# One decoder layer on one core: sixteen instead of eight of the 32 hidden tiles of the second feed-forward product by seven products of quarters

## The chip, the core and the metric

The kernel runs on one core of one Trainium2 chip. The metric is the device time of one launch in microseconds (us). Engines are named as the profile names them: PE is TensorE (PEld its weight loads), DVE is VectorE, ACT is ScalarE, POOL is GpSimd, SP is SyncE, on which every DMA of this kernel is issued.

## The reference, cut to what matters

The layer mixes tokens (a gated unit and sparse attention), attends to 256 memory tokens, and ends in a dense feed-forward block, which is what the change touches. There are 512 tokens of width 1024 and 4096 hidden columns, all float32:

```python
h = rms_norm(x, norm_ffn_g[l])
x = x + jnp.square(jax.nn.relu(h @ w_ff1[l])) @ w_ff2[l]
```

## The kernel before

Every float32 operand of a product is split into a rounded part `hi` and a remainder `lo` (`split_any`: a cast on ACT or DVE, then a subtraction on DVE), and a product is three matmuls: hi·hi, hi·lo, lo·hi.

The 4096 hidden columns are 32 tiles `f` of 128. The first product writes them transposed (`hid[f]`, 128 hidden columns by 512 tokens). Tiles 4 to 31 of the first product are already made in groups of four by `seven`.

The second product (stage `ff2`) has two ways. **Plain**: `load_ff2` loads 128 rows of `w_ff2` into a `raw` buffer and splits them and `hid[f]`; `part` adds the tile's product to eight accumulators in PSUM (`accs`: four token tiles by two column halves). One tile is 24 matmuls that stream 512 columns each. **By quarters**: eight hidden tiles at once. `quarters` cuts their 1024 hidden columns by 512 tokens into four quarters a11, a12, a21, a22 and makes seven split operands from them: A11, A12, A22 themselves, and S1 = a21+a22, S2 = S1−a11, S3 = a11−a21, S4 = a12−S2. `seven` then runs, for each half `g` of the output columns, seven products instead of eight (24 matmuls of 256 columns each, by `prod2`). It forms sums of the weight quarters (`either_tt`, DVE or POOL) and splits them (`pair`), adds the products up from PSUM on DVE (`u2`, `v`), and hands four results to `sink`, which multiplies by the row factor `rf[t]`, adds to the residual and stores to `out`.

Tiles 8 to 15 (`SEVEN = 8`) go by quarters, the 24 others plain, in the sequence `order`. The quarters are prepared after the twelfth plain tile. At the end come the plain tiles' accumulators, added to the residual `xr`, and then the two groups `fg0` and `fg1`.

Buffers come from shared pools: `b8` has 12 buffers of 8 KB a partition, `w` four (split weights), `raw` three, `P` six and `bT` two of 512 columns. A hidden tile or an operand in a `b8` buffer must have been read for the last time before the next one gets it.

Nothing runs in the order of the code. `Plan` records all operations and `schedule` lays them out per engine in advance. Among the operations that could start first on an engine it takes the one with the smallest due number, which is its place in the code, shifted by `LEADS` of its stage. Engines then run their rows strictly in that order, so a row that waits holds back all behind it, on SP too.

Of the kernel before, what the change touches and what calls it, by code (L numbers as in the profile page):

```python
# [9 lines left out]
F32 = mybir.dt.float32  # L10
# [4 lines left out]
OP = mybir.AluOpType  # L15
AX = mybir.AxisListType

P = 128
# [19 lines left out]
SEVEN = 8  # L38
# [19 lines left out]
         "wa": dict(w=3, raw=2),  # L58
         "wf": dict(w=1, raw=1)}

LEADS = {"ch_f0": -4441, "ch_f1": 6232, "ch_norm0": -2300, "ch_norm1": -2363, "ch_norm2": 367,
# [9 lines left out]
         "ln": -7310, "masks": -496, "mem": -4549, "mix": -620, "mk": -3102, "mkv": -2398,  # L71
# [10 lines left out]


class Plan:
# [338 lines left out]
def hybrid_block(ctx, tc, x, mem, norm_mix_g, w_in, sg_ln_g, sg_ln_b, sg_w, sg_b, q_norm_g,  # L423
# [66 lines left out]
    def split_any(src, hi, lo):  # L490

        nc.either(("scalar", "copy"), ("vector", "tensor_copy"))(hi, src)
        dve.tensor_tensor(lo, src, hi.bitcast(F32), OP.subtract)
# [869 lines left out]
    def hid_tiles(f):  # L1363

        if f < 2:
            return [zpool.tile([P, 512], F32, tag="bT", bufs=2, name=nm("hid")) for _ in range(2)]
        if f < 8:
            return [zpool.tile([P, 512], F32, tag="P", bufs=6, name=nm("hid")) for _ in range(6)]
        if f < 20:
            t = b8([P, 4, T], F32)  # L1370
            hid4[f] = t
            return [t[:, i, :] for i in range(4)]
        t = [zpool.tile([P, 2, 512], F32, tag="q", bufs=5, name=nm("hid")) for _ in range(1 if f == 28 else 2)]
        if f == 28:
            g = cpool.tile([P, 2, 512], F32, tag="gain", bufs=1, name=nm("hid"))
            nc.home[g.tensor.name] = "gain"
            t.append(g)
        return [v[:, i, :] for v in t for i in range(2)]

    def hid_tile(f):  # L1380
# [42 lines left out]
    def half(t, i):  # L1423
        return t[:, i, :].rearrange("p (k n) -> p k n", k=4)

    def either_tt(out, a, b, op):
        nc.either(("vector", "tensor_tensor"), ("gpsimd", "tensor_tensor"))(out, a, b, op)
# [127 lines left out]
            start=f == order[0], stop=f == order[-1])  # L1555


    def quarters():
        t = b8([P, 2, 1024], F32)
        nc.stage = "fs"  # L1560
        a11, a12, a21, a22 = (hid4[SEVEN + 4 * kh][:, :, th * 2 * P:th * 2 * P + 2 * P]
                              for th in range(2) for kh in range(2))

        def parts(src, name):
            nc.stage = f"fs.{name}"
            w = b8([P, 2, 1024], F32R)
            h = half(w, 0), half(w, 1)
            split_any(src, *h)
            return h

        A11 = parts(a11, 0)
        either_tt(half(t, 0), a21, a22, OP.add)
        S1 = parts(half(t, 0), 1)
        either_tt(half(t, 1), half(t, 0), a11, OP.subtract)
        S2 = parts(half(t, 1), 2)
        either_tt(half(t, 0), a11, a21, OP.subtract)
        S3 = parts(half(t, 0), 3)
        A12 = parts(a12, 4)
        either_tt(half(t, 0), a12, half(t, 1), OP.subtract)
        S4 = parts(half(t, 0), 5)  # L1580
        A22 = parts(a22, 6)
        return t, (A11, A12, None, A22, S1, S2, S3, S4)

# [10 lines left out]
                nc.tensor.matmul(o, al[:, k, c], wh[:, k, :], **dict(on, stop=i == 1 and k == 3))  # L1594


    order = [*range(20, 28), *range(SEVEN), *range(SEVEN + 8, 20), *range(28, 32)]
    for n, f in enumerate(order[:-LAST]):
        nc.stage = "ff2"
        load_ff2(f)  # L1600
        for t in range(TT):
            for blk in range(2):
                part(f, t, blk)
        if n == 11:
            tq, quads = quarters()
    nc.stage = "ff2"
    for f in order[-LAST:]:
        load_ff2(f)
    nc.stage = "xr"
    xr = [b8([P, 2, D], F32) for _ in range(2)]  # L1610
    for t in range(TT):
        dma(xr[t // 2][:, t % 2, :], xq[t])
    nc.stage = "ff2"
    for t in range(TT):
        for blk in range(2):
            for f in order[-LAST:]:
                part(f, t, blk)
            xv = xr[t // 2][:, t % 2, blk * 512:blk * 512 + 512]
            dve.scalar_tensor_tensor(xv, accs[2 * t + blk], rf[t], xv, OP.mult, OP.add)

    for g in range(2):
        def load_w(kh, ch):
            t = raw4()
            c = g * 512 + ch * 2 * P
            dma(t.rearrange("p (k n) -> p k n", k=4), w2v[:, SEVEN + 4 * kh:SEVEN + 4 * kh + 4, c:c + 2 * P])
            return t

        def sink(src, th, ch):
            for i in range(2):
                t = 2 * th + i  # L1630
                c = g * 512 + ch * 2 * P
                xv = xr[t // 2][:, t % 2, c:c + 2 * P]
                dve.scalar_tensor_tensor(xv, src[:, i * 2 * P:i * 2 * P + 2 * P], rf[t], xv, OP.mult, OP.add)
                dma(out[0, t * P:t * P + P, c:c + 2 * P], xv)

        seven(f"fg{g}", load_w, tq[:, g, :], prod2, quads, [bank() for _ in range(4)], sink)
    nc.issue()


# [29 lines left out]
```

## Time and profile before

| | |
|---|---|
| time, median of 3 runs | 680.83 us (680.05 to 682.28) |
| profiled execution: its time, its span | 681.13 us, 679.4 us |
| PE busy | 670.3 us, 99% |
| DVE busy | 527.9 us, 78% |
| ACT busy | 360.2 us, 53% |
| POOL busy | 79.3 us, 12% |
| mean granted clock of TensorE | 0.999 |

The span runs from the first to the last instruction, and the 1.7 us to the time lie around it. A matmul's duration in the profile holds its way through the array, so durations of neighbours overlap; busy time counts an overlap once. The feed-forward part fills the second half: its first product ends at about 504 us, the plain tiles of the second end at 635.4 us, and the two groups by quarters at 675.7 us.

### The profile page before, as it was taken

Reading aid. Unit: us, or ns where it says so; the run is one execution under the profiler, and the core shown is the slowest. Engines: PE = TensorE matmul, PEld = TensorE weight load, DVE = VectorE, ACT = ScalarE, POOL = GpSimd, SP = SyncE. Lnnn points to the kernel's source line nnn. Section 1 sums busy time; section 2 is a strip of 40 time slices with the busy share of each in tenths; the row PEclk is TensorE's granted clock in tenths of the full one; section 3 lists DMA queues with packets and bytes.
Section 4 is the critical chain, followed back from the end, with each engine's and each line's share of the span. In section 5 each row is a group of like instructions: output and inputs, shape, how many; then the busy total and the mean of one; then the engine's idle time right before and its main releaser. Section 6 shows DMA issues by size and latency. Waiting matters only on the chain.

```text
span 679.4 us, 11076 instructions
## 1 busy us (share of the span) xinstructions
PE 670.3 (99%) x4232; PEld 601.8 (89%) x4232; DVE 527.9 (78%) x940; ACT 360.2 (53%) x690; POOL 79.3 (12%) x123
## 2 busy tenths in 40 slices
PE   8999999899999999999999999999999999999997
PEld 7898888788989898898899999999998888888997
DVE  6688889898989996578899979888998344444695
ACT  5444576786877784566635645456583221121330
POOL 2001211053343230031200000000000000000000
PEclk9999999999999999999999999999999999999999
DMA  8633465451111210305332334433253623222231
GB/s 257 201 89 107 142 180 182 157 185 63 63 64 63 67 53 9 122 1 156 125 94 63 114 105 124 124 94 113 74 170 110 217 93 94 93 94 93 73 115 63
DMA packets 54453, 74.80 MB, mean 110 GB/s; under 512 B 3392, under 2 KB 38720, under 8 KB 54400
## 3 DMA queue, kind: packets, MB, share of 16 engines
q1 hardware_dynamic: 54400, 74.10, 34.9%
q8 instruction: 33, 0.54, 0.3%
q14 instruction: 20, 0.16, 0.1%
HBM read 69.89 MB, written 4.19 MB: 109 GB/s over the span
## 4 chain that ended last, share of the span: by engine, by line
PE 93%; DMA 2%; DVE 2%; ACT 1%; POOL 0%; issue 0%; SPq 0%; DVEq 0%; ACTq 0%; POOLq 0%
PE ps L419 93%; DMA raw<-in_cmp_w_dram 2%; DVE b L419 1%; DVE w L419 1%; DMA b<-in_x_dram 1%; ACT w L419 1%; ACT L419 0%; POOL P L419 0%; ACT b L419 0%; SPq L419 0%; ACT pc L419 0%; DVE q L419 0%; DVE P L419 0%; DVEq L1664 0%; DVE pt L419 0%
## 5 line engine op out<-in xcount | busy, mean ns | idle before, releaser
L419 PE MATMUL ps<-w,b 128*128 128x512 f32 (+3 forms) x1312 | 261.7, 353 | 0.5 <-DVE w L419 0.5
L419 PEld LDWEIGHTS ps<-w,b 128*128 128x128 f32 (+1 forms) x1312 | 210.2, 188 | 29.8 <-DVE w L419 1.0
L419 ACT CAST w<-raw 128x1024 fp32r<-128x1024 f32 (+1 forms) x89 | 90.9, 1022 | 132.0 <-PE ps L419 124.3
L419 PE MATMUL ps<-b,w 128*128 128x256 f32 (+1 forms) x1224 | 152.8, 287 | 0.0
L419 PEld LDWEIGHTS ps<-b,w 128*128 128x128 f32 x1224 | 150.3, 192 | 1.9
L419 DVE TENSOR_TENSOR w<-raw,w 128x1024 fp32r<-128x1024 f32 (+2 forms) x109 | 127.9, 1174 | 27.1 <-ACT w L419 26.2
L419 PE MATMUL ps<-w,q 128*128 128x512 f32 x624 | 148.4, 392 | 0.0
L419 PEld LDWEIGHTS ps<-w,q 128*128 128x128 f32 x624 | 116.0, 188 | 23.2
L419 DVE TENSOR_TENSOR b<-ps,b 128x512 fp32r<-128x512 f32 (+2 forms) x88 | 54.2, 637 | 9.1 <-ACT b L419 8.7
L419 ACT CAST b<-ps 128x512 fp32r<-128x512 f32 (+2 forms) x88 | 46.0, 546 | 20.2 <-PE ps L419 19.8
L419 PE MATMUL ps<-b,b 128*128 128x256 f32 (+1 forms) x344 | 54.1, 288 | 0.0
L419 ACT CAST w<-b 128x1024 fp32r<-128x1024 f32 x21 | 22.0, 1049 | 49.4 <-PE ps L419 37.2
L419 PEld LDWEIGHTS ps<-b,b 128*128 128x128 f32 x344 | 46.4, 190 | 2.0 <-DVE b L419 0.2
L419 POOL TENSOR_SCALAR P<-P,s,gates 128x128 f32<-128x128 f32 (+3 forms) x57 | 35.6, 633 | 69.7 <-DVE s L419 65.4
L419 DVE TENSOR_TENSOR w<-b,w 128x1024 fp32r<-128x1024 f32 x27 | 32.9, 1220 | 10.9 <-ACT w L419 10.8
L419 ACT ACTIVATE P<-P,s 128x128 f32<-128x128 f32 (+3 forms) x64 | 35.7, 559 | 6.9 <-DVE s L419 6.7
L419 DVE TENSOR_TENSOR z<-ps,z 128x512 f32<-128x512 f32 (+2 forms) x54 | 34.7, 646 | 4.5 <-PE ps L419 4.0
L419 POOL TENSOR_TENSOR b<-raw,b 128x1024 f32<-128x1024 f32 x1 | 2.4, 2400 | 278.3 <-DVE w L419 278.3
L419 PE MATMUL ps<-b,q 128*128 128x256 f32 (+2 forms) x144 | 33.3, 343 | 0.0
L419 PE MATMUL ps<-idf,P 128*128 128x128 f32 x192 | 31.8, 275 | 0.5 <-POOL P L419 0.5
L419 POOL TENSOR_TENSOR r<-s,negh 128x1 f32<-128x1 f32 (+2 forms) x25 | 19.6, 784 | 108.8 <-DVE s L419 108.8
L419 DVE CUSTOM_DVE_ANT_0 P<-ps,tri 128x128 f32<-128x128 f32 (+3 forms) x64 | 28.8, 482 | 1.4 <-PE ps L419 1.1
(166 smaller groups left out, 667.9 us busy)
## 6 DMA issues: line engine op xcount, KB each, us to landing
raw<-in_w_ff_dram SPq DMA_DIRECT2D x64, 512.0 KB, 3.8
raw<-in_w_in_dram SPq DMA_DIRECT2D x12, 512.0 KB, 3.7
raw<-in_cmp_w_dram SPq DMA_DIRECT2D x8, 512.0 KB, 5.0
raw<-in_w_out_dram SPq DMA_DIRECT2D x8, 512.0 KB, 3.5
raw<-in_w_mkv_dram SPq DMA_DIRECT2D x8, 512.0 KB, 3.6
b<-in_x_dram SPq DMA_DIRECT2D x8, 256.0 KB, 6.0
raw<-in_w_in_dram SPq DMA_DIRECT2D x8, 256.0 KB, 6.2
b<-in_x_dram SPq DMA_DIRECT2D x4, 512.0 KB, 4.3
```

The lines of the kernel that those rows point to most:

```text
L419: getattr(getattr(self.nc, eng), op)(*a, **k)
```

## The change

The second product takes tiles 16 to 23 by quarters too. `quarters(f)` and the groups run for f = 8 and f = 16, so there are four groups (`fg8`, `fg9`, `fg16`, `fg17`) and 16 plain tiles. The first set's operands are prepared after the sixth plain tile. The second set's stand in the code behind the first group. Tiles 20 to 23 lie in two buffers of two tiles each, so an operation on their quarters becomes two of 512 columns (`pieces`). The residual no longer waits in two `b8` buffers; it lies in eight of 512 columns (`bT`, `P`) and is loaded by eight DMAs instead of four. The sums of the groups with f = 8 stay in these buffers, those with f = 16 go to `out`. `LEADS` is another table.

```diff
-LEADS = {"ch_f0": -4441, "ch_f1": 6232, "ch_norm0": -2300, "ch_norm1": -2363, "ch_norm2": 367,
...
+LEADS = {"ch_f1": -603, "ch_f2": -578, "ch_f3": -4970, "ch_norm2": 876, "ch_o0": -494, "ch_o0.w0.2": -1640,
...
-    def quarters():
+    def quarters(f):
+
         t = b8([P, 2, 1024], F32)
-        nc.stage = "fs"
-        a11, a12, a21, a22 = (hid4[SEVEN + 4 * kh][:, :, th * 2 * P:th * 2 * P + 2 * P]
+        a11, a12, a21, a22 = ([(k, v[:, :, th * 2 * P:th * 2 * P + 2 * P]) for k, v in hid4[f + 4 * kh]]
                               for th in range(2) for kh in range(2))
...
+        def tt(out, a, b, op):
+            for o, x, y in pieces(out, a, b):
+                either_tt(o, x, y, op)
+
         A11 = parts(a11, 0)
-        either_tt(half(t, 0), a21, a22, OP.add)
-        S1 = parts(half(t, 0), 1)
...
+        tt(t0, a21, a22, OP.add)
+        S1 = parts(t0, 1)
+        tt(t1, t0, a11, OP.subtract)
+        S2 = parts(t1, 2)
...
-    order = [*range(20, 28), *range(SEVEN), *range(SEVEN + 8, 20), *range(28, 32)]
+    order = [*range(SEVEN + 16, 28), *range(SEVEN), *range(28, 32)]
...
-        if n == 11:
-            tq, quads = quarters()
+        if n == 5:
+            tq, quads = quarters(SEVEN)
...
-    xr = [b8([P, 2, D], F32) for _ in range(2)]
+    xr = [[zpool.tile([P, 512], F32, tag=tag, bufs=n, name=nm("xr")) for _ in range(2)]
+          for tag, n in (("bT", 2), ("P", 6), ("P", 6), ("P", 6))]
     for t in range(TT):
-        dma(xr[t // 2][:, t % 2, :], xq[t])
+        for blk in range(2):
+            dma(xr[t][blk], xq[t][:, blk * 512:blk * 512 + 512])
...
+    for f in (SEVEN, SEVEN + 8):
+        for g in range(2):
+            def load_w(kh, ch):
+                t = raw4()
                 c = g * 512 + ch * 2 * P
-                xv = xr[t // 2][:, t % 2, c:c + 2 * P]
-                dve.scalar_tensor_tensor(xv, src[:, i * 2 * P:i * 2 * P + 2 * P], rf[t], xv, OP.mult, OP.add)
-                dma(out[0, t * P:t * P + P, c:c + 2 * P], xv)
...
+            def sink(src, th, ch):
+                for i in range(2):
+                    t = 2 * th + i
+                    c = ch * 2 * P
+                    xv = xr[t][g][:, c:c + 2 * P]
+                    dve.scalar_tensor_tensor(xv, src[:, i * 2 * P:i * 2 * P + 2 * P], rf[t], xv, OP.mult, OP.add)
+                    if f > SEVEN:
+                        dma(out[0, t * P:t * P + P, g * 512 + c:g * 512 + c + 2 * P], xv)
+
+            seven(f"fg{f + g}", load_w, tq[:, g, :], prod2, quads, [bank() for _ in range(4)], sink)
+            if f == SEVEN and g == 0:
+                tn, next_quads = quarters(f + 8)
+        tq, quads = tn, next_quads
```

On PE, the rows behind the last plain tile of before are whole products of 24 matmuls (the weights `w_...` of one product, the operand `b_...` of the hidden columns, the bank `ps_...`):

```order
L419 MATMUL ps_1169<-w_1248,q_1249 128x512 x3
L419 MATMUL ps_1252<-w_1258,b_1103_1207 128x256 x24
L419 MATMUL ps_1253<-w_1260,b_1104_1208 128x256 x24
L419 MATMUL ps_1254<-w_1262,b_1105_1209 128x256 x24
L419 MATMUL ps_1255<-w_1264,b_1106_1210 128x256 x24
L419 MATMUL ps_1252<-w_1267,b_1107_1211 128x256 x24
L419 MATMUL ps_1253<-w_1268,b_1108_1212 128x256 x24
```

At the same place of the changed kernel the products of group `fg8` (banks 1234 to 1237) and, further down, of `fg9` (1261 to 1264) lie in pieces between each other:

```order
L422 MATMUL ps_1169<-w_1224,q_1225 128x512 x3
L422 MATMUL ps_1234<-w_1240,b_1085_1189 128x256 x24
L422 MATMUL ps_1235<-w_1242,b_1086_1190 128x256
L422 MATMUL ps_1236<-w_1244,b_1087_1191 128x256
L422 MATMUL ps_1237<-w_1246,b_1088_1192 128x256 x24
L422 MATMUL ps_1236<-w_1244,b_1087_1191 128x256 x23
L422 MATMUL ps_1234<-w_1249,b_1089_1193 128x256 x24
L422 MATMUL ps_1235<-w_1242,b_1086_1190 128x256 x13
L422 MATMUL ps_1261<-w_1267,b_1085_1189 128x256
L422 MATMUL ps_1235<-w_1242,b_1086_1190 128x256 x10
L422 MATMUL ps_1261<-w_1267,b_1085_1189 128x256 x23
L422 MATMUL ps_1262<-w_1269,b_1086_1190 128x256
```

So 192 matmuls of 512 columns are gone ahead of this place, 336 matmuls of 256 columns stand behind it, and a product's first matmul often stands alone among those of another.

On DVE, between the first and the second group of before (`fg0` and `fg1`), these rows stand: weight sums and remainders (`w`, `raw`, `b_1102_1206`), sums of products (`z`), and updates of the residual (`b_1146`, `b_1147`):

```order
L419 TENSOR_TENSOR w_1270<-b_1102_1206,w_1270 128x1024
L419 TENSOR_TENSOR b_1102_1206<-raw_1276,raw_1275 128x1024
L419 TENSOR_TENSOR z_1265<-ps_1255,z_1265 128x512
L419 TENSOR_TENSOR w_1277<-raw_1275,w_1277 128x1024
L419 SCALAR_TENSOR_TENSOR b_1147_1251<-z_1265,rf_950,b_1147_1251 128x256
L419 SCALAR_TENSOR_TENSOR b_1146_1250<-ps_1252,rf_897,b_1146_1250 128x256
L419 SCALAR_TENSOR_TENSOR b_1146_1250<-ps_1252,rf_924,b_1146_1250 128x256
L419 SCALAR_TENSOR_TENSOR b_1147_1251<-z_1265,rf_965,b_1147_1251 128x256
```

In the changed kernel, in the second group (`fg9`), the rows are these, where `b_1149_1253` is the scratch tile of the second set, `b_1153`, `b_1154` and `b_1155` its operands S3, A12 and S4, and `hid_1087`, `hid_1088` hidden tiles 20 to 23:

```order
L422 TENSOR_TENSOR b_1153_1257<-b_1149_1253,b_1153_1257 128x1024
L422 TENSOR_TENSOR w_1271<-b_1084_1188,w_1271 128x1024
L422 TENSOR_TENSOR w_1273<-raw_1266,w_1273 128x1024
L422 TENSOR_TENSOR b_1084_1188<-raw_1275,b_1084_1188 128x1024
L422 TENSOR_TENSOR b_1154_1258<-hid_1087,b_1154_1258 128x512
L422 TENSOR_TENSOR b_1154_1258<-hid_1088,b_1154_1258 128x512
L422 TENSOR_TENSOR b_1149_1253<-hid_1087,b_1149_1253 128x512
L422 TENSOR_TENSOR b_1149_1253<-hid_1088,b_1149_1253 128x512
L422 TENSOR_TENSOR w_1276<-raw_1275,w_1276 128x1024
L422 TENSOR_TENSOR b_1155_1259<-b_1149_1253,b_1155_1259 128x1024
L422 TENSOR_TENSOR z_1251<-ps_1235,z_1245 128x512
L422 TENSOR_TENSOR w_1277<-raw_1270,w_1277 128x1024
```

Here six rows of the second set stand among those that the running groups need. Its operands A11, S1 and S2 stand further up, among the plain tiles, and A22 further down.

On SP, the loads of the residual now stand one by one among the loads of the plain tiles' weights:

```order
L422 DMA raw_1214<-in_w_ff_dram 128x1024
L422 DMA xr_1230<-xq_749 128x512
L422 DMA raw_1217<-in_w_ff_dram 128x1024
L422 DMA xr_1231<-xq_749 128x512
L422 DMA raw_1220<-in_w_ff_dram 128x1024
L422 DMA xr_1232<-xq_750 128x512
L422 DMA raw_1223<-in_w_ff_dram 128x1024
L422 DMA xr_1233<-xq_750 128x512
L422 DMA raw_1238<-in_w_ff_dram 128x4x256
```

Before, four loads of 128 x 1024 stood there, ahead of the weight loads of the last twelve plain tiles; now each waits for a buffer that a hidden tile leaves.

## Rows read from the trace of the kernel before

**Rows 1.** The page: span, then busy us of each engine.

```profile
span 679.4 us, 11076 instructions
...
PE 670.3 (99%) x4232; PEld 601.8 (89%) x4232; DVE 527.9 (78%) x940; ACT 360.2 (53%) x690; POOL 79.3 (12%) x123
```

**Rows 2.** The chain that ended last: start, us and name of its longest piece.

```profile
200.13 475.57 PE ps L419 x3092
```

**Rows 3.** Whom PE waited for in the whole span: us, times, longest.

```profile
PE ps L419 <- DMA b<-in_x_dram: 1.4, 1, 1.4
PE ps L419 <- DVE pc L419: 1.2, 1, 1.2
PE ps L419 <- DVE zero L419: 1.1, 1, 1.1
PE ps L419 <- DVE b L419: 0.7, 2, 0.6
PE ps L419 <- POOL P L419: 0.5, 1, 0.5
PE ps L419 <- DVE w L419: 0.5, 1, 0.5
```

**Rows 4.** Busy time of each engine by stretch.

```profile
core 0: us, PE busy (x) PEld busy (x) DVE busy (x) ACT busy (x) POOL busy (x), PEclk, DMA share, GB/s
0.00:200.00 200.00, 194.72 (x1140) 167.97 (x1140) 166.29 (x408) 130.62 (x285) 44.42 (x75) 1.00 0.46 141
...
330.00:471.00 141.00, 141.00 (x1104) 137.48 (x1103) 126.04 (x142) 75.94 (x127) 3.74 (x5) 1.00 0.33 101
...
540.00:635.40 95.40, 95.40 (x423) 79.04 (x422) 41.28 (x52) 18.12 (x18) 2.40 (x1) 1.00 0.27 89
635.40:675.70 40.30, 40.28 (x336) 40.08 (x335) 32.79 (x42) 12.74 (x14) 0.00 (x0) 1.00 0.32 98
```

**Rows 5.** Groups by shape, 520 to 680 us: count, busy us, mean ns of one.

```profile
L419 PE MATMUL ps<-w,q 128*128 128x512 f32 x432 | 98.1, 389 | 0.0
...
L419 DVE SCALAR_TENSOR_TENSOR b<-z,rf,b 128x256 f32<-128x256 f32 x12 | 5.3, 480 | 0.1
```

**Rows 6.** DVE in order of time, inside the two groups by quarters.

```profile
636.08 1.22 DVE L419 TENSOR_TENSOR w<-b,w 128x1024 fp32r<-128x1024 f32 x1
637.21 1.22 DVE L419 TENSOR_TENSOR w<-raw,w 128x1024 fp32r<-128x1024 f32 x1
...
653.26 0.68 DVE L419 TENSOR_TENSOR z<-ps,z 128x512 f32<-128x512 f32 x1
653.87 1.22 DVE L419 TENSOR_TENSOR b<-raw,b 128x1024 f32<-128x1024 f32 x1
655.00 0.87 DVE L419 SCALAR_TENSOR_TENSOR b<-z,rf,b 128x256 f32<-128x256 f32 x2
655.79 0.68 DVE L419 TENSOR_TENSOR z<-ps,z 128x512 f32<-128x512 f32 x1
```

**Rows 7.** The one POOL subtraction of the feed-forward end, and DVE beside it.

```profile
626.97 2.40 POOL L419 TENSOR_TENSOR b<-raw,b 128x1024 f32<-128x1024 f32 x1 [278.33 <-DVE w L419]
627.47 0.74 DVE L419 SCALAR_TENSOR_TENSOR b<-ps,rf,b 128x512 f32<-128x512 f32 x1
```

**Rows 8.** DMA issues: count, KB each, median us to landing.

```profile
raw<-in_w_ff_dram SPq DMA_DIRECT2D x64, 512.0 KB, 3.8
...
b<-xq SPq DMA_DIRECT2D x4, 512.0 KB, 5.6
```

**Rows 9.** PE and ACT at the start, in order of time.

```profile
5.95 0.68 ACT L419 ACTIVATE b<-ps,gT 128x512 fp32r<-128x512 f32 x1
...
6.83 0.66 PE L419 MATMUL ps<-idf,b 128*128 128x128 f32 x4 [1.36 <-DMA b<-in_x_dram]
...
7.24 4.53 PE L419 MATMUL ps<-w,b 128*128 128x512 f32 x18
```

More of the change, by code (lines that the diff above doesn't have):

```diff
@@ L59 @@
          "wf": dict(w=1, raw=1)}
-LEADS = {"ch_f0": -4441, "ch_f1": 6232, "ch_norm0": -2300, "ch_norm1": -2363, "ch_norm2": 367,
[9 rows of a table removed]
-         "ln": -7310, "masks": -496, "mem": -4549, "mix": -620, "mk": -3102, "mkv": -2398,
[10 rows of a table removed]
+LEADS = {"ch_f1": -603, "ch_f2": -578, "ch_f3": -4970, "ch_norm2": 876, "ch_o0": -494, "ch_o0.w0.2": -1640,
[23 rows of a table added]
 class Plan:
@@ L1370, in hid_tiles @@
             t = b8([P, 4, T], F32)
-            hid4[f] = t
+            hid4[f] = [(0, t)]
             return [t[:, i, :] for i in range(4)]
@@ L1377, in hid_tiles @@
             t.append(g)
+        else:
+            hid4[f] = [(0, t[0]), (2, t[1])]
         return [v[:, i, :] for v in t for i in range(2)]
@@ L1555, in part, with pieces @@
             start=f == order[0], stop=f == order[-1])
-    def quarters():
+    def quarters(f):
         t = b8([P, 2, 1024], F32)
-        nc.stage = "fs"
-        a11, a12, a21, a22 = (hid4[SEVEN + 4 * kh][:, :, th * 2 * P:th * 2 * P + 2 * P]
+        a11, a12, a21, a22 = ([(k, v[:, :, th * 2 * P:th * 2 * P + 2 * P]) for k, v in hid4[f + 4 * kh]]
                               for th in range(2) for kh in range(2))
+        t0, t1 = ([(0, half(t, i))] for i in range(2))
+        def pieces(*srcs):
+            ks = sorted({k for s in srcs for k, _ in s}) + [4]
+            for k, e in zip(ks, ks[1:]):
+                r = []
+                for s in srcs:
+                    b, v = max((x for x in s if x[0] <= k), key=lambda x: x[0])
+                    r.append(v[:, k - b:e - b, :])
+                yield r
         def parts(src, name):
-            nc.stage = f"fs.{name}"
+            nc.stage = f"fs{f}.{name}"
             w = b8([P, 2, 1024], F32R)
             h = half(w, 0), half(w, 1)
-            split_any(src, *h)
-            return h
+            for x, hi, lo in pieces(src, *([(0, v)] for v in h)):
+                split_any(x, hi, lo)
+            return h
+        def tt(out, a, b, op):
+            for o, x, y in pieces(out, a, b):
+                either_tt(o, x, y, op)
         A11 = parts(a11, 0)
-        either_tt(half(t, 0), a21, a22, OP.add)
-        S1 = parts(half(t, 0), 1)
[L1574 to L1577, printed above, removed]
+        tt(t0, a21, a22, OP.add)
+        S1 = parts(t0, 1)
+        tt(t1, t0, a11, OP.subtract)
+        S2 = parts(t1, 2)
+        tt(t0, a11, a21, OP.subtract)
+        S3 = parts(t0, 3)
         A12 = parts(a12, 4)
-        either_tt(half(t, 0), a12, half(t, 1), OP.subtract)
-        S4 = parts(half(t, 0), 5)
+        tt(t0, a12, t1, OP.subtract)
+        S4 = parts(t0, 5)
         A22 = parts(a22, 6)
@@ L1617, in hybrid_block @@
                 part(f, t, blk)
-            xv = xr[t // 2][:, t % 2, blk * 512:blk * 512 + 512]
+            xv = xr[t][blk]
             dve.scalar_tensor_tensor(xv, accs[2 * t + blk], rf[t], xv, OP.mult, OP.add)
[L1621 to L1630, printed above, removed]
-                c = g * 512 + ch * 2 * P
-                xv = xr[t // 2][:, t % 2, c:c + 2 * P]
-                dve.scalar_tensor_tensor(xv, src[:, i * 2 * P:i * 2 * P + 2 * P], rf[t], xv, OP.mult, OP.add)
-                dma(out[0, t * P:t * P + P, c:c + 2 * P], xv)
-        seven(f"fg{g}", load_w, tq[:, g, :], prod2, quads, [bank() for _ in range(4)], sink)
+    for f in (SEVEN, SEVEN + 8):
+        for g in range(2):
+            def load_w(kh, ch):
+                t = raw4()
+                c = g * 512 + ch * 2 * P
+                dma(t.rearrange("p (k n) -> p k n", k=4), w2v[:, f + 4 * kh:f + 4 * kh + 4, c:c + 2 * P])
+                return t
+            def sink(src, th, ch):
[10 more added lines that the diff above has]
+        tq, quads = tn, next_quads
     nc.issue()
```

42 rows, old and new, of the table LEADS are left out of this document.

## The prediction

> **What bounds the kernel now.** I read the page first: PE is busy for 670.3 of 679.4 us [rows 1]. A share near 100% can still hide waits, since a matmul's duration covers its way through the array, so I asked the chain of waits next. Its longest piece is PE alone, 475.6 us from 200.1 us on without a break [rows 2], which takes in the whole feed-forward block. The list of PE's waits agrees: six kinds, 5.4 us together [rows 3], all of them in the first 200 us or just behind. The table by stretch shows the rest [rows 4]. From 330 to 471 us, where the first product runs by seven products, PE is busy 141.0 of 141.0 us, at the full granted clock (1.00), while DVE is busy 126.0 us (89%). In the plain tiles up to 635.4 us DVE needs 41.3 of 95.4 us (43%), and in the two groups by quarters 32.8 of 40.3 us (81%). The clock is at its upper level, 2.4 GHz, in every stretch shown. So only PE's own rows set the end, and time is won by taking columns off PE, as long as DVE keeps up.
>
> **The product, removed and added.** Eight hidden tiles leave the plain way: 8 x 24 = 192 matmuls of 512 columns. The group by shape has 432 of these in 98.1 us [rows 5], 227.1 ns each when overlaps are counted once (the mean of 389 ns counts them twice). Removed: 192 x 0.2271 = 43.6 us. Added are two groups of seven products of 24 matmuls of 256 columns, 336. Exactly as many run behind 635.4 us in the kernel before, in 40.28 us [rows 4], 119.9 ns each. Added: 40.3 us. The product gains **3.3 us**. It is less than the eighth by which the multiplications shrink (5.5 of 43.6 us), because a matmul of half the width takes 53% of the time, not 50%.
>
> The Trainium skill, TensorE: Matmul & The Clock Gate, section Back-to-back issue gap, gives N/2.4 ns plus about 2.5 ns between isolated matmuls of N columns. By it the two widths would be 215.8 and 109.2 ns and the gain 41.4 − 36.7 = 4.7 us. The trace doesn't agree (227.1 and 119.9 ns), and the measurement decides.
>
> **DVE and ACT behind the plain tiles.** The groups' stretch doubles to 4 x 168 = 672 matmuls, 80.6 us. In the order of the changed kernel I counted DVE's rows behind the last update from the plain accumulators: 40 tensor-tensor rows of 1024, 26 of 512, 32 residual updates of 256. From start to start such rows take 1.13 us (636.08 to 637.21), 0.61 us (653.26 to 653.87) and 0.395 us (two in 0.79 from 655.00) [rows 6]. Sum: 45.2 + 15.9 + 12.6 = 73.7 us. The same count of before (17, 10, 16) gives 31.6 us where the table shows 32.8, so I add 3.7%: 76.4 us, 95% of PE's 80.6. That is tighter than before, but it fits. If instead each row held DVE for its whole duration (1.22, 0.68 and 0.48 us [rows 5, 6]), the sum would be 81.9 us, 1.3 us over.
>
> The tightest place is from DVE's row that adds up the end of `fg8`'s S2 product to its row for the end of `fg9`'s S4 product. The list of rows of `fg9` shown above lies in it, with S3, A12 and S4 of the second set. There are 34 rows (15 of 1024, 11 of 512, 8 of 256): 16.9 + 6.7 + 3.2 = 26.8 us, with the 3.7% 27.8 us, by full durations 29.6 us. PE's 236 matmuls there take 28.3 us. So DVE ends between 1.5 us early and 1.3 us late, and nearer to early, since starts, not durations, set the pace in every row I could read. The pieces into which PE's products are cut have little reserve against a late remainder. I charge **0.3 us** for small waits, between 0 (as from 330 to 471 us, at 89% of DVE) and 2.6 (both overruns).
>
> The other rows of the second set (A11, S1, S2, about 7.5 us) stand among the plain tiles, where DVE has over half its time free; without that cover they would come on top of the 76.4 us and PE would wait for some 3 us. ACT gets seven casts more for the second set and one for each pair, but has 12.7 of 40.3 us busy in the groups [rows 4] and stays far from the bound.
>
> **Loads and residual.** The weights' bytes are the same: eight loads of 512 KB for eight tiles, or eight for two groups. The residual is the same 2 MB in eight loads rather than four. A load of weights lands in 3.8 us, one of the residual in 5.6 us [rows 8]; a plain tile takes 24 x 0.2271 = 5.45 us on PE, and three `raw` buffers stand ahead of it. Cost nothing, as long as a residual load doesn't stop SP (rival below). The last stores are the same rows as before, so what follows PE's end stays.
>
> **The other table of leads.** It reorders every engine. Behind 200 us PE has nothing to win. Ahead of it the 5.4 us of waits include 1.1 us for the first operand of all, so at most 4.3 us could come back; a loss isn't bounded by the trace, and I take once the largest wait seen (1.4 us) as its size. One place can be read: PE stands 1.36 us for the second slice of x until 6.83 us, and only then, after four transposes, starts its first products at 7.24 us [rows 9]. In the new order three products of the first slice stand ahead of these transposes. Their operand is written by ACT from 5.95 us for 0.68 us, so they can start near 6.7 us. I take **0.3 us** of gain, and 0 for all else.
>
> **Sum.** −3.3 + 0.3 − 0.3 = −3.3 us. From the profiled execution's 681.13 us that is 677.8 us. That execution lay 0.3 us over the median of 680.83, so for a median I say 677.5 us, 0.5% faster. About 0.3% (2.0 us) is what a measurement of this kernel can tell from no change.
>
> **Rivals.**
> (1) *DVE becomes the bound of the groups.* For it: 95% by starts, 102% by durations. Against it: 89% without a wait in the first product. It would give back 1.3 to 2.6 us: 678.8 to 680.1 us.
> (2) *POOL stops DVE in the tight stretch.* The new order has two POOL subtractions behind the plain tiles' sums instead of one: the old one beside the last plain tiles, and one in `fg16`'s preparation, next to the end of the stretch above. One takes 2.40 us, and before, DVE's update from PSUM ran beside it at its usual 0.74 us [rows 7]. The rows behind it that matter most have PSUM operands too. If rows with two SBUF operands came to stand beside it and had to wait, PE would be late by 2.4 less the 0.5 to 1.5 us in hand: 678.4 to 679.4 us. The Trainium skill, SBUF — State Buffer, section Who interferes with whom, says that a DVE instruction with two SBUF inputs and a GpSimd one that reads SBUF exclude each other, and that the later one stands still until the first is done. The one pair in these rows has a PSUM operand and ran undisturbed, as the page has it; no row here shows the other kind.
> (3) *The residual's loads hold SP* (slower). Each waits for a hidden tile's buffer, and weights queue behind it. With three `raw` buffers PE has about two plain tiles, 10.9 us, in hand; a load held longer than that stops PE by about a tile for each tile of delay. At one tile, 5.45 us: 683.0 us. For it: four residual loads alternate with the last four weight loads of the plain tiles. Against it: the tiles that leave these buffers are split well ahead of their products, as DVE has over half its time free there.
> (4) *The new order opens other waits in the first 200 us*, or closes more. One more of the largest kind gives 678.9 us; half of the 4.3 us closed gives 675.4.
>
> **Chances.** Forecast, with the product's gain mostly whole and the order neutral or better (675.4 to 678.7 us): 0.72. Rival 1: 0.11. Rival 2: 0.05. Rival 4's loss: 0.08. Rival 3: 0.04. The range leaves out rival 3 and thin ends of the others: 675.7 to 680.2 us. Faster by over 0.3%, below 678.8 us: the forecast and some of rivals 2 and 4, 0.74. Same: 0.21. Slower: 0.05.
>
> **What would show it.** Right: PE busy near 667 us with the same six kinds of waits; plain tiles that end near 592 us and groups of 80.6 to 81 us behind them without PE waits over 0.3 us; DVE near 92 to 95% there. Wrong: PE waits for `w` or for DVE's reads of `ps` between `fg9` and `fg16` (rivals 1, 2), PE waits for `w` among the last plain tiles with SP held by `xr` (rival 3), or a first product by quarters that starts at another time than 43.6 us earlier, less what changed ahead of it (rival 4). A width that costs other than 227 and 120 ns would upset the largest term.

## Result, and the profile after

The changed kernel takes 677.38 us (median of ten runs, 676.16 to 679.81), the kernel before 681.96 us on the same chip (ten runs, 680.05 to 683.8). The ratio is 0.9937, with a 95% interval from 0.9919 to 0.9956: 0.6% faster. The forecast was 677.5 us. Its largest term came out, but that the time was met to 0.1 us is partly luck: the measured gain is 4.6 us, where 3.3 us were forecast from a lower start.

The profiled execution of the changed kernel took 679.81 us, the longest of its ten, and a second one, shown below, 676.3 us. Where they part is told under the experiments. The page of the profiled one, which answers to [rows 1]:

```profile
span 678.0 us, 11433 instructions
...
PE 669.6 (99%) x4376; PEld 609.3 (90%) x4376; DVE 557.5 (82%) x972; ACT 369.0 (54%) x708; POOL 85.8 (13%) x127
```

DVE is busy 29.6 us more, PE 0.7 us less (666.8 us in the second execution; the forecast had some 667). The waits of PE over the whole span, as in [rows 3] (us, times, longest):

```profile
PE ps L422 <- ACT b L422: 1.8, 1, 1.8
PE ps L422 <- DVE pc L422: 1.3, 1, 1.3
PE ps L422 <- DVE zero L422: 1.1, 1, 1.1
PE ps L422 <- DVE b L422: 0.5, 1, 0.5
```

The waits for POOL's `P` and DVE's `w` of before are gone, and the wait for the load of x has become one of 1.8 us for ACT. The chain of waits shows where the last of them lies (start, us, name):

```profile
135.09 539.19 PE ps L422 x3660
674.28 0.02 issue
```

Before, PE's unbroken piece began at 200 us [rows 2]; now it begins at 135 us, and the four groups lie inside it. The table by stretch, columns as in [rows 4], has the four groups in its first row here and the tightest stretch of the prediction in its second:

```profile
593.60:674.30 80.70, 80.66 (x673) 80.46 (x671) 75.12 (x98) 31.46 (x35) 2.40 (x1) 1.00 0.31 99
...
602.40:630.80 28.40, 28.40 (x239) 28.40 (x239) 27.12 (x35) 14.02 (x17) 2.12 (x1) 1.00 0.30 96
```

The groups last 80.70 us where two of them lasted 40.30 [rows 4], and PE works in 80.66 us of it. DVE is busy 93% of that stretch, and 27.12 of 28.40 us in the tightest part. The groups of rows by shape, as in [rows 5], from 510 to 680 us:

```profile
L422 PE MATMUL ps<-w,b 128*128 128x256 f32 x672 | 80.8, 283 | 0.0
L422 PE MATMUL ps<-w,q 128*128 128x512 f32 x240 | 54.6, 389 | 0.0
```

54.6 us by 240 is 227.5 ns, 80.8 us by 672 is 120.2 ns: the two widths cost what the prediction took. DVE at the end of the tightest part, in order of time (start, us; idle time ahead of a row in brackets), with POOL's one subtraction inside the groups:

```profile
627.33 1.22 DVE L422 TENSOR_TENSOR b<-raw,raw 128x1024 f32<-128x1024 f32 x1
628.46 0.87 DVE L422 SCALAR_TENSOR_TENSOR xr<-ps,rf,xr 128x256 f32<-128x256 f32 x2
629.25 0.68 DVE L422 TENSOR_TENSOR z<-ps,z 128x512 f32<-128x512 f32 x1
630.75 0.69 DVE L422 TENSOR_TENSOR z<-ps,z 128x512 f32<-128x512 f32 x1 [0.81 <-PE ps L422]
...
628.68 2.40 POOL L422 TENSOR_TENSOR raw<-raw,raw 128x1024 f32<-128x1024 f32 x1 [41.09 <-ACT w L422]
```

At 630.75 us DVE waits 0.81 us for PE, not PE for DVE. That is what DVE has in hand there. POOL's subtraction lies beside rows that read PSUM, and they keep their 0.87 us for two and 0.68 us for one.

### The profile page after: what moved, and what is told of

It reads as the page before. It is cut to its first block, busy times and chain, and to the rows that moved or that the text cites. A ratio compares the mean times of both kernels' runs of the same rounds, so it can differ in the third digit from the quotient of the medians.

```text
span 678.0 us, 11433 instructions
## 1 busy us (share of the span) xinstructions
PE 669.6 (99%) x4376; PEld 609.3 (90%) x4376; DVE 557.5 (82%) x972; ACT 369.0 (54%) x708; POOL 85.8 (13%) x127
## 4 chain that ended last, share of the span: by engine, by line
PE 98%; DMA 1%; DVE 0%; ACT 0%; issue 0%; SPq 0%; DVEq 0%
PE ps L422 98%; DMA raw<-in_w_in_dram 1%; DVE b L422 0%; ACT b L422 0%; ACT L422 0%; SPq L422 0%; DVE s L422 0%; DVE xr L422 0%; ACT pc L422 0%; DVEq L1692 0%; DVE pc L422 0%; ACT w L422 0%
## 5 line engine op out<-in xcount | busy, mean ns | idle before, releaser
L422 PE MATMUL ps<-w,b 128*128 128x512 f32 (+3 forms) x1648 | 305.3, 341 | 1.8 <-ACT b L422 1.8
L422 PEld LDWEIGHTS ps<-w,b 128*128 128x128 f32 (+1 forms) x1648 | 252.2, 190 | 31.6 <-ACT b L422 2.2
L422 ACT CAST w<-raw 128x1024 fp32r<-128x1024 f32 (+2 forms) x81 | 82.3, 1021 | 75.9 <-PE ps L422 69.4
L422 PE MATMUL ps<-w,q 128*128 128x512 f32 x432 | 103.3, 392 | 0.0
L422 PEld LDWEIGHTS ps<-w,q 128*128 128x128 f32 x432 | 80.1, 188 | 15.9
L422 ACT CAST w<-b 128x1024 fp32r<-128x1024 f32 x29 | 30.4, 1050 | 66.0 <-PE ps L422 43.4
L422 PE MATMUL ps<-b,b 128*128 128x256 f32 x344 | 53.3, 286 | 0.0
L422 DVE TENSOR_TENSOR w<-b,w 128x1024 fp32r<-128x1024 f32 x33 | 40.3, 1221 | 9.6 <-ACT w L422 9.4
L422 DVE TENSOR_TENSOR b<-b,b 128x1024 fp32r<-128x1024 f32 (+2 forms) x31 | 36.3, 1195 | 3.2 <-ACT b L422 3.0
L422 DVE CAST w<-raw 128x1024 fp32r<-128x1024 f32 (+2 forms) x28 | 18.3, 653 | 22.9 <-PE ps L422 22.3
```

Source lines behind the costliest of these rows:

```text
L422: getattr(getattr(self.nc, eng), op)(*a, **k)
```

## Experiments

Ratios are against the kernel before on the same chip in the same session, with 95% intervals.

**Each kernel once more.** The two kernels unchanged, each profiled in one further execution, in another session.

> The kernel before, unchanged, profiled once more. Theory 3 (the clock at the start is chance from one execution to the next): the stretch of 1.2 GHz ends somewhere else than at 5.3 us, up to 13.5 us, and the span is longer by what it costs there. Rival (it belongs to the order of the rows): 5.3 us again, within 0.5.

> The changed kernel, unchanged, profiled once more. Theory 3: the first products run at 227 ns from another time than 13.4 us on, and the span is shorter by up to 3.1 us. Rival (it belongs to the order): 427 ns to about 13.4 us again.

The kernel before took 681.06 us (681.13 the first time), the changed kernel 676.3 us (679.81). The chains of waits, before and changed:

```profile
199.90 475.73 PE ps L419 x3092
675.65 0.48 DVE b L419
```

```profile
131.63 539.13 PE ps L422 x3660
670.76 0.03 issue
```

The changed kernel's last piece is as long as the first time (539.13 and 539.19 us) but starts 3.46 us earlier. The whole difference of its executions lies ahead of 135 us, and it begins with the first product. PE in the profiled execution and in the second one, and ACT in both:

```profile
7.32 2.08 PE L422 MATMUL ps<-w,b 128*128 128x512 f32 x4 [1.82 <-ACT b L422]
9.19 1.91 PE L422 MATMUL ps<-idf,b 128*128 128x128 f32 x8
...
6.06 0.62 ACT L422 CAST w<-raw 128x512 fp32r<-128x512 f32 x1 [1.41 <-DMA raw<-in_w_in_dram]
6.58 0.68 ACT L422 ACTIVATE b<-ps,gT 128x512 fp32r<-128x512 f32 x1
```

```profile
6.04 1.30 PE L422 MATMUL ps<-w,b 128*128 128x512 f32 x4 [0.86 <-ACT b L422]
7.17 1.04 PE L422 MATMUL ps<-idf,b 128*128 128x128 f32 x8
...
4.78 0.62 ACT L422 CAST w<-raw 128x512 fp32r<-128x512 f32 x1
5.30 0.68 ACT L422 ACTIVATE b<-ps,gT 128x512 fp32r<-128x512 f32 x1
```

The activation that PE needs stands behind a cast on ACT, and the cast waits for the first weights' load. In the first execution it began 1.28 us later than in the second, where no wait for a load is named. PE then not only started later; its first four matmuls of products took 2.08 instead of 1.30 us, and the eight transposes behind them 1.91 instead of 1.04 us. So the same program begins at a lower pace of PE in one execution and at a higher one in another. The table by stretch gives a granted clock of 1.00 in both, so the clock isn't shown as the reason here; in three kernels further down, those with no sums on POOL, with all sums on it and with one remainder twice, a slow start stands beside 0.50 to 0.51 from 7.5 to 10.5 us. The kernel before started alike both times: its first 18 matmuls of products took 4.53 us [rows 9] and 4.70.

The two executions lie at the ends of what was seen. In the eleven profiled executions with the new table (these two and those of the experiments below, one of them with a longer warm-up) the first product begins between 6.04 and 7.32 us, the middle one at 6.72 us.

In the second execution PE ends at 670.76 us and in that of before at 675.63: 4.87 us, of which 3.3 is the product. The other 1.6 us lie ahead of it, and the early start of this execution is part of them.

**The table of leads, by halves.** One kernel is the changed one with the old leads for all stages ahead of the feed-forward block, the other the kernel before with the new leads.

```diff
-LEADS = {"ch_f1": -603, "ch_f2": -578, "ch_f3": -4970, "ch_norm2": 876, "ch_o0": -494, "ch_o0.w0.2": -1640,
+LEADS = {"ch_f0": -4441, "ch_f1": 6232, "ch_norm0": -2300, "ch_norm1": -2363, "ch_norm2": 367,
...
```

> The changed kernel, but with the old leads for every stage ahead of the feed-forward block and the new ones from there on. Theory 1 (the gain is PE's columns): the groups end as in the changed kernel, plain tiles end 43.6 us earlier than before, 3.3 us under the kernel before: ratio 0.995. Theory 2 (the gain is mostly the new order of the first 330 us): ratio 0.998 to 1.000.

> The kernel before (8 tiles by quarters) with the new leads. Theory 1: PE's columns are those of before, so what is left is the order of the first 330 us, by the trace of the changed kernel 1.4 us better behind 14 us and 0 to 3 us worse ahead of it: ratio 0.998 to 1.002. Theory 2: ratio 0.994 to 0.996.

With the old leads ahead: 680.51 us, 0.9982 (0.9968 to 0.9996). By the ratio alone that is what was expected if the gain were mostly the new order. The rows don't bear this out: the groups take 80.67 us, as in the changed kernel, so the product's gain is there. What is lost lies ahead of them. The old waits are back, and a new one stands where the two tables meet:

```profile
PE ps L423 <- DVE w L423: 1.4, 2, 0.9
...
PE ps L423 <- DMA b<-in_x_dram: 0.9, 1, 0.9
...
PE ps L423 <- POOL P L423: 0.5, 1, 0.5
```

The medians of the changed kernel and of this one lie 3.1 us apart (677.38 and 680.51; other sessions of before differ by 0.01 us), of which this joint, at 371.8 us, is 0.9. So in the medians the leads ahead of the feed-forward block carry some 2 us, more than the prediction gave them; the two intervals leave about 1.6 us of doubt on that, and the changed kernel's own 4.6 us less the product's 3.3 leave them 1.3. Waits account for about half: apart from the one for the first load, and from the joint, PE waits 4.0 us here and 2.9 us in the changed kernel. For the rest only the start can be named, and only in the profiled execution: PE's first 18 matmuls of products took 5.80 us, 1.3 us more than before.

The kernel before with the new leads: 684.07 us, 1.0039 (1.0024 to 1.0055), slower and outside both expected ranges. Its PE ends at 675.4 us, about where that of before does, but then DVE has this left:

```profile
674.59 1.42 DVE L421 TENSOR_TENSOR z<-ps,z 128x512 f32<-128x512 f32 x2 [3.92 <-PE ps L421]
675.92 1.66 DVE L421 SCALAR_TENSOR_TENSOR b<-z,rf,b 128x256 f32<-128x256 f32 x4
677.50 0.69 DVE L421 TENSOR_TENSOR z<-ps,z 128x512 f32<-128x512 f32 x1
678.22 0.88 DVE L421 SCALAR_TENSOR_TENSOR b<-z,rf,b 128x256 f32<-128x256 f32 x2
```

Before, one pair of updates from 675.72 us ended the kernel. The new leads order the last products otherwise when there are two groups, so this run tells nothing clean of the start; it shows that a table made for one program is no gain to this other one. The same holds for all kernels below: they keep the table of the changed kernel, and what they would lose with one of their own was not tried. Their losses may be larger than they need be.

**A longer warm-up.** The changed kernel with 44 instead of 28 matmuls on zeros at its start.

```diff
-NWARM = 28
+NWARM = 44
```

> The changed kernel with 44 instead of 28 warm-up matmuls of zeros ahead of the first transpose. Theory 3 (the changed kernel loses up to 3 us at the start in those executions in which TensorE runs its first products at 1.2 GHz, 427 ns for 512 columns instead of 227): with PE busy to about 5.8 us the first products run at 227 ns in the profile, and the time is 0.5 to 2.5 us under the changed kernel: ratio 0.990 to 0.993. Rival (the clock at the start is chance, whatever PE did): 427 ns may be seen again, ratio 0.993 to 0.995, the cost of the later transposes included.

678.09 us, 0.9948 (0.9934 to 0.9963), the same as the changed kernel within the intervals. In its profile the first three matmuls of products take 0.97 us, the higher pace, though PE waits 1.23 us ahead of them; but 0.5 us come back as a wait for DVE's `z` at 440 us. The residual's kernel below has the same pace with 28 matmuls on zeros, its first four in 1.30 us behind a wait of 1.21 us, and neither the pace nor a gain in the median is shown to come from the longer warm-up.

**How much DVE has in hand.** Four kernels add rows to DVE in the groups. The first computes the groups' weight sums on DVE alone (one was on POOL); the second computes one remainder of the second set twice; the third all seven of them; the fourth as the third, with no sum on POOL in the groups and the preparations.

```diff
     def either_tt(out, a, b, op):
+        if nc.stage.startswith("fg"):
+            dve.tensor_tensor(out, a, b, op)
+            return
```

```diff
                 split_any(x, hi, lo)
+                if f > SEVEN and name == 5:
+                    dve.tensor_tensor(lo, x, hi.bitcast(F32), OP.subtract)
```

The third and fourth have `f > SEVEN` alone as the condition.

> The changed kernel with the one weight sum on POOL inside the groups computed on DVE. DVE then has 41 rows of 1024 there, 74.9 us by starts, 77.6 us with the 3.7 per cent, 96 per cent of PE. If the 0.8 us in hand at the tightest place stay, as that row lies behind it: groups 80.6 us, ratio 0.993. If not: one PE wait of up to 1 us, ratio 0.994 to 0.996.

> The changed kernel with one more DVE row of 1024 in the groups (the remainder of the second set's S4 computed twice): 1.13 us more on DVE, against 0.8 us in hand at the tightest place. If DVE has just that much in hand: one PE wait of 0.3 to 1.5 us in the groups, ratio 0.994 to 0.997. If an overload of any size also brings stretches at 1.2 GHz, as with seven rows more: groups 83 us or more, ratio above 0.998. If nothing is that tight: groups 80.6 us, ratio 0.993.

> The changed kernel with each remainder of the second set of quarters computed twice on DVE (seven operands; dead work). DVE's rows behind the plain tiles' sums are then 43 of 1024, 28 of 512, 32 updates and 2 casts: 79.5 us by starts, 81 us with the 2% that the profile of the changed kernel shows on top of such a sum. Theory 1 with a DVE at 93% of the groups: the reserve is used up, PE waits of 0.3 to 1.5 us in all appear behind the plain tiles, ratio 0.994 to 0.996. Rival (DVE has ample reserve there): no PE wait, ratio 0.9937. Rival (each row holds DVE for its whole duration): 7 us over, ratio 1.000 or more.

> As e4_dve7 (each remainder of the second set computed twice, dead work), but every sum of the second product on DVE, none on POOL. In e4 two POOL subtractions of 512 columns took 7.0 us while DVE ran rows with two SBUF operands without a break, PE then stood for 2.1 and 2.9 us and ran two stretches at 1.2 GHz. Theory 4 (e4 lost its 9.9 us over the changed kernel mostly because POOL was held off by DVE, and by the clock that followed): DVE's rows sum to 81.8 us by starts, 83.4 with 2%, so the groups take 83 to 85 us and the ratio is 0.996 to 1.000. Rival (DVE's own rows are the cause): the groups take over 90 us again, ratio 1.007 or more.

The table gives the four groups from the end of the plain tiles to PE's last matmul, all from the tables by stretch, with two further kernels that are told below.

| kernel | groups, us | DVE busy | PE busy | ratio |
|---|---|---|---|---|
| changed | 80.70 | 75.12 | 80.66 | 0.9937 (0.9919 to 0.9956) |
| no sums on POOL | 80.88 | 75.75 | 80.88 | 0.9965 (0.9953 to 0.9977) |
| one remainder twice | 87.02 | 79.89 | 83.28 | 1.0039 (1.0027 to 1.005) |
| seven remainders twice | 91.63 | 82.66 | 85.95 | 1.0082 (1.0063 to 1.0102) |
| the same, no sums on POOL | 90.49 | 83.58 | 84.32 | 1.0074 (1.0047 to 1.01) |
| residual in large buffers | 92.84 | 84.38 | 85.03 | 1.0104 (1.0083 to 1.0126) |
| all sums on POOL | 91.12 | 76.46 | 85.30 | 1.0087 (1.0058 to 1.0115) |

Without POOL's sum the tightest part still holds (same columns as above):

```profile
592.40:673.28 80.88, 80.88 (x672) 80.48 (x671) 75.75 (x98) 30.43 (x34) 0.00 (x0) 1.00 0.31 98
601.16:629.56 28.40, 28.40 (x239) 28.40 (x239) 27.93 (x35) 14.04 (x16) 0.00 (x0) 1.00 0.30 96
```

DVE is busy 27.93 of 28.40 us and PE never waits in the groups. So 0.8 us more than in the changed kernel (27.12) is carried there, with half a microsecond left. The median of this kernel, 679.62 us, is 2.2 us above that of the changed one all the same. Some 1 us of it lies in its order: the groups take 0.2 us more, and behind PE's last matmul DVE has rows left for 1.8 us (until 675.11), in the changed kernel for 0.9 us. DVE's last rows in this kernel and in the changed one:

```profile
672.84 0.69 DVE L422 TENSOR_TENSOR z<-ps,z 128x512 f32<-128x512 f32 x1 [1.87 <-PE ps L422]
...
674.63 0.48 DVE L422 SCALAR_TENSOR_TENSOR xr<-ps,rf,xr 128x256 f32<-128x256 f32 x1
```

```profile
674.30 0.88 DVE L422 SCALAR_TENSOR_TENSOR xr<-ps,rf,xr 128x256 f32<-128x256 f32 x2 [0.31 <-PE ps L422]
```

The chain of its profiled execution also has PE's last piece from 133.75 us on, 2.1 us later than in the changed kernel's second execution: 0.5 us by a later first product, and the rest by PE's next 355 matmuls from there on, which took 67.60 instead of 65.95 us with a granted clock of 0.51 from 7.5 to 10.5 us. Whether that belongs to this kernel or to the execution stays open; its ten runs lie between 679.0 and 680.7 us.

One remainder twice is the first to break. It isn't one row alone: the planner, seeing DVE and ACT otherwise, also gave DVE the sum from POOL and three casts from ACT, so that DVE has 103 rows for 98 and 4.8 us more. Where that went, in stretches:

```profile
591.78:678.80 87.02, 83.28 (x672) 82.21 (x671) 79.89 (x103) 28.30 (x32) 0.00 (x0) 0.98 0.30 93
626.00:630.00 4.00, 2.96 (x21) 2.49 (x20) 4.00 (x8) 1.74 (x2) 0.00 (x0) 1.00 0.02 4
...
645.00:649.00 4.00, 1.31 (x9) 0.91 (x8) 4.00 (x6) 1.04 (x1) 0.00 (x0) 1.00 0.01 3
649.00:652.00 3.00, 3.00 (x17) 3.00 (x17) 3.00 (x4) 0.00 (x0) 0.00 (x0) 0.54 0.11 17
```

DVE's 79.89 us would still fit under 80.66 us of PE's, yet the groups last 6.3 us longer. DVE is busy without a gap where PE stands still, at 626 and at 645 us. From 652 to 656 us it is busy for 1.41 of 4 us again, but idle time behind a late product doesn't bring it back. And behind the second stop the granted clock is 0.54, the level of 1.2 GHz, for 3 us in which PE gets through 17 matmuls instead of 25. 3.7 of the 6.3 us are waits (87.02 − 83.28). The other 2.6 us are more busy time of PE for the same matmuls. The lower clock is about 1 us of that in the 3 us shown, and single matmuls between two stops add to it, since their whole duration shows (0.38 us each at 626.74 and 646.76 us, where one costs 0.12 us in the stream). The two overloads with all remainders show the same, at 9.8 and 10.9 us. The expected 0.994 to 0.996 for seven remainders was far off: it had counted on DVE's free time in all, and left out the clock. Its rival of whole durations has a ratio that fits (1.000 or more), but not the rows: DVE is busy for 82.66 us, near the 81 us by starts, where whole durations would come to some 88.

**POOL beside DVE.** The kernel with seven remainders has two POOL subtractions of 512 columns in the groups. POOL, then DVE beside it:

```profile
616.56 6.97 POOL L422 TENSOR_TENSOR b<-hid,b 128x512 f32<-128x512 f32 x2 [30.31 <-DVE b L422]
```

```profile
618.68 1.22 DVE L422 TENSOR_TENSOR w<-raw,w 128x1024 fp32r<-128x1024 f32 x1
619.82 1.29 DVE L422 TENSOR_TENSOR b<-hid,b 128x512 fp32r<-128x512 f32 x2
...
622.31 2.30 DVE L422 TENSOR_TENSOR w<-b,w 128x1024 fp32r<-128x1024 f32 x1 [0.50 <-ACT w L422]
```

Two rows of 512 took 6.97 us, where one of 1024 takes 2.40 [rows 7], and a DVE row 2.30 instead of 1.22 us. This is rival 2's mechanism: the DVE row from 622.31 us ends 1.1 us behind POOL's last, at 624.61 and 623.53 us, as if it had begun only then. The Trainium skill, SBUF — State Buffer, section Who interferes with whom, has it that a DVE row with two SBUF inputs and a GpSimd row that reads SBUF shut each other out; these rows agree. But taking it away gains nothing here: without any sum on POOL the same overload gives 687.51 us against 687.33, with four rows more on DVE (109 for 105). The opposite was tried too, all sums of the groups on POOL (`pool.tensor_tensor` in the edit above):

> The changed kernel with all 20 weight sums of the four groups on POOL (48 us at 2.4 us each). DVE's rows fall to some 60 us. If POOL and DVE rows with two SBUF operands exclude each other: 48 us of POOL beside some 45 us of such DVE rows don't fit into 80.6 us, POOL rows last longer than 2.4 us in the profile, PE waits, ratio above 1.005. If they run side by side: no waits, ratio 0.992 to 0.995.

```profile
603.19 2.41 POOL L422 TENSOR_TENSOR b<-raw,raw 128x1024 f32<-128x1024 f32 x1 [4.94 <-DMA raw<-in_w_ff_dram]
605.67 3.26 POOL L422 TENSOR_TENSOR raw<-raw,raw 128x1024 f32<-128x1024 f32 x1
...
615.31 3.32 POOL L422 TENSOR_TENSOR b<-raw,b 128x1024 f32<-128x1024 f32 x1 [2.63 <-DVE w L422]
```

688.92 us, 1.0087. DVE has 85 rows instead of 98 but is busy 76.46 us, 1.3 us more, where some 60 us were expected. PE waits 5.8 us in the groups, 4.7 of them for split weights (`w`), which are made from the sums; a sum takes up to 3.32 us here where DVE takes 1.13. With this table POOL doesn't help out.

**The residual's buffers.** The changed kernel with the residual in two `b8` buffers, as before.

```diff
-    xr = [[zpool.tile([P, 512], F32, tag=tag, bufs=n, name=nm("xr")) for _ in range(2)]
-          for tag, n in (("bT", 2), ("P", 6), ("P", 6), ("P", 6))]
+    xb = [b8([P, 2, D], F32) for _ in range(2)]
+    xr = [[xb[t // 2][:, t % 2, blk * 512:blk * 512 + 512] for blk in range(2)] for t in range(TT)]
```

> The changed kernel with the residual in two 8 KB buffers again, as before the change. The operands A11, S1 and S2 of the second set then find no free buffer among the plain tiles and are made behind them: DVE has 45 rows of 1024, 26 of 512, 32 updates of 256 and three casts in the groups, 81.7 us by starts against 80.6 us of PE. The theory that the small residual buffers are what lets the change gain (DVE has to fit under PE): PE waits of 1 to 5 us appear between 592 and 675 us, groups of 82 to 86 us, ratio 0.998 to 1.008. The rival that the product's columns alone decide: groups of 80.6 us, ratio 0.993 as the changed kernel.

688.58 us, 1.0104 (1.0083 to 1.0126). The operands A11, S1 and S2 of the second set no longer find buffers among the plain tiles, DVE has 107 rows behind them instead of 98, and PE stops:

```profile
628.08 11.29 PE L422 MATMUL ps<-w,b 128*128 128x256 f32 x71 [2.19 <-DVE z L422]
642.37 3.02 PE L422 MATMUL ps<-w,b 128*128 128x256 f32 x23 [3.00 <-DVE w L422]
```

The groups last 92.84 us, more than the 82 to 86 expected: behind the first of these waits the granted clock is 0.50 to 0.54 from 628 to 634 us. So the part of the change that moves no work of PE is worth 12.1 us of the groups with this table of leads; without it the saved columns turn into a loss. The rival that the columns alone decide falls.

**A third set.** Twenty-four tiles by quarters, eight plain; the two lines that matter of the edit:

```diff
-    order = [*range(SEVEN + 16, 28), *range(SEVEN), *range(28, 32)]
+    order = [*range(SEVEN)]
...
-    for f in (SEVEN, SEVEN + 8):
+    for f in (SEVEN, SEVEN + 8, SEVEN + 16):
```

> Twenty-four tiles by quarters in three sets, eight plain. By PE's columns alone another 3.3 us would be won: groups of 120.9 us behind plain tiles that end near 548 us, ratio near 0.989. By DVE's rows (about 133 us by starts behind the plain tiles, against 121 us of PE) DVE is the bound: groups of 130 us or more, waits of PE for w, z or b throughout, some stretches at 1.2 GHz, ratio 1.005 to 1.03.

```profile
548.07:693.08 145.01, 128.56 (x1009) 126.00 (x1007) 134.96 (x171) 50.57 (x57) 4.19 (x2) 0.95 0.26 84
609.00:616.00 7.00, 2.35 (x10) 2.15 (x11) 7.00 (x9) 0.97 (x2) 0.00 (x0) 0.62 0.31 101
```

699.87 us, 1.0258 (1.0228 to 1.0288). DVE is now the bound, busy 134.96 of 145.01 us, against 133 forecast by starts; PE waits 16.4 us and runs at 0.95. In this form, and with this table, two sets are as many as DVE carries.

## Why the prediction was right, point by point

**The time: met, in part by luck.** The forecast took 3.3 us from 680.83 us, the median of three runs of before. Ten runs have 681.96 us, and against these the changed kernel gains 4.6 us. A start that was 1.1 us low and a gain that was 1.3 us small stood against each other.

**The product, −3.3 us: right.** 40.4 us were added (80.70 less 40.30) where 40.3 were forecast, 43.5 us left (98.1 [rows 5] less 54.6) where 43.6 were, and the durations of both widths held (227.5 and 120.2 ns). The Trainium skill's formula for isolated matmuls (TensorE: Matmul & The Clock Gate, Back-to-back issue gap) gave an estimate of 4.7 us; these widths, each with its own weight load, don't follow it.

**Small waits in the groups, +0.3 us: measured 0.** PE waits nowhere behind 135 us. DVE's 76.4 us (95%) came out as 75.12 us (93%), and the tightest part as 27.12 of 28.40 us where 27.8 of 28.3 were forecast. Rows cost their distance from start to start; the sum by full durations (81.9 us) is refuted by the same 75.12 us. So rival 1 didn't happen. The experiments say how near it was: 0.8 us more in the tightest part is carried, 4.8 us more over the groups is not. Where they missed is the price. The prediction had about 3 us of waits if A11, S1 and S2 lost their cover among the plain tiles; the kernel that takes it away lost 12.1 us in the groups, since PE's waits (7.8 us) also bring stretches at the lower clock.

**The start, −0.3 us: the place held on the whole, its reason did not.** The first product was to begin near 6.7 us, from the activation at 5.95 us [rows 9]. It began at 7.32 us in the profiled execution and at 6.04 in the second, and at 6.72 us in the middle one of all eleven. The step had taken the activation's time over from before and not asked what stands ahead of it on ACT: a cast that waits for the first weights' load, which lands at another time in each execution. It also left out the pace of the first products, which varies by more than the term: four of them took 1.30 to 2.08 us.

**Everything else ahead of the groups, 0: this term was too small.** Apart from the wait for the first load, PE waits 4.0 us in the kernel before [rows 3] and 2.9 us in the changed one; in the second executions 4.1 and 3.2 us. So about 1 us of waits came back, which the sum put at 0 though it had seen that up to 4.3 us could. With the product's 3.3 us that is 4.2 to 4.4 of the 4.6 us gained. The kernel with the old leads, some 2 us slower apart from its joint, points the same way. In the profiled execution the late and slow start took this back and more: PE ends at 674.28 us, 1.4 us earlier than the 675.70 of before [rows 4], 3.3 less 1.9. Of the signs named in advance, PE's 667 us are so missed in that execution (669.6) and met in the second (666.8), and of the six kinds of waits three are gone and one is new.

**Rivals 2 to 4.** POOL and DVE do hold each other up, but only in kernels that add rows or move sums, and with seven remainders it isn't what decides. Of rival 3 there is no trace: PE has no wait among the plain tiles. Of rival 4 the better side came in part: about 1 us of waits closed, where it had 2.15 us. Its worse side, other waits opened, isn't seen: what made the profiled execution late is the start, which differs from one execution to the next.

## What to carry to other kernels

When work is taken off an engine that is never idle and given to one that is 80% busy, count the second engine's rows by their starts, in the tightest stretch and not over the whole; 27.9 of 28.4 us was still free of waits here, and a sum of 79.9 us in 80.7 was not. A buffer moved to make an operand's preparation start earlier can be worth more than the work saved: 12.1 us against 3.3, with one table of leads. Of a reordering, count the waits that it can close, check what the first row waits for on its own engine, and take a second execution before reading differences of a few microseconds at the start. And take a small difference from as many runs of the kernel before as of the changed one: the first three of before lay 1.1 us under ten.

## What the runs showed of the hardware

One program's first microseconds differ between executions by more than the product gains here (3.3 us): by 3.46 us between two executions of the changed kernel, with the first four matmuls of 512 columns in 2.08 or in 1.30 us, and a granted clock that reads 1.00 in both. In another execution, of the kernel without sums on POOL, where PE had been idle for 1.54 us ahead of the first product, the profile shows the clock itself:

```profile
7.50:10.50 3.00, 3.00 (x12) 2.66 (x13) 1.95 (x4) 1.49 (x3) 0.00 (x0) 0.51 1.11 341
```

In the residual's kernel, idle for 1.21 us at the same place, it reads 1.00 there.

A short stop of PE can cost more than its length: behind 645 to 649 us, in which PE was busy for 1.31 us, it was granted 0.54 for the next 3 us. And POOL's subtraction has no fixed price: half of the 2.40 us of [rows 7] would be 1.2 us for 512 columns, and beside DVE rows that read SBUF twice it was 3.5.
